# Moving the sample states' loads, copies and outer products inside the second feed-forward stage, and the normalisation's pinned steps at the end

## The chip, the cores and the metric

The kernel runs on one core of one Trainium2 chip. The time is device microseconds (us) of one execution of the whole program. TensorE (PE) multiplies matrices, with its weight loads shown as a row of their own (PEld); VectorE (DVE), ScalarE (ACT) and GpSimd (POOL) compute elementwise; SyncE (SP), ACT and POOL issue DMA transfers. Each engine works through its own instructions in order, and engines wait for each other by semaphores.

## The reference

One layer of a decoder for 512 new prompt tokens and 8 sample tokens (one new token for each of 8 sequences). With `h` the residual stream (1024 features):

```python
h = h + 0.5 * swiglu(rms_norm(h, ffn1_norm), w_gate, w_up, w_down)      # FFN 1, 2816 wide
h = h + hybrid_mixer(rms_norm(h, mix_norm), ...)                         # pooling and state-space mixer
h = h + 0.5 * swiglu(rms_norm(h, ffn2_norm), w_gate, w_up, w_down)      # FFN 2
y = rms_norm(h, final_norm)
```

The mixer keeps a state for each sample sequence b and each of 16 heads, of 64 x 128 numbers (1024 rows of 128 for each b). One step of it is

```python
new_state = exp(dt * A) * old_state + outer(dt * x, B)      # per sequence and head
```

The output `new_ssm_sample` is this new state, 4 MB of float32 for all 8 sequences; nothing later in the step reads it. All outputs are float32.

## The kernel before

**Layout.** Features lie on the 128 partitions and the 520 tokens (512 prompt, 8 sample) in the free dimension, cut in two halves of 260 (`HALVES`, `HB`). A float32 operand is split into a high part (fp32r) and a low rest, and one product is three matmuls (`mm3`, lines 122, 125 and 126). The two FFNs also save one of eight sub-products by a seven-product scheme (Strassen's).

**An FFN's steps.** The class `Ffn` works through 22 blocks of 128 hidden features in four chunks. For each chunk it takes the gate and up products of its blocks (tiles named `A_k` and `BE_k`, weights `raw`, `whi`, `wlo`, `shi`, `slo`), and then the down products of the chunk, two output blocks at a time (the same names with `1d` or `2d`: four down tiles for each of the first three chunks). Below, a "gate tile" is a step with 7 x 12 matmul groups and a "down tile" one with 7 x 9. The border of a chunk is where its last gate tile gives way to its first down tile.

`step(k)` (line 426 on) writes one tile: product 1, a call of `state()`, product 4 of the tile before, then products 5, 6, 3, 7 and 2, with another `state()` after product 3. Products 1, 6, 7 and 4 pile up in one PSUM bank (`A`), products 5 and 3 in another (`BE`); between them ACT copies the running sum out (`ac`, line 361), and the next product of that bank may not start before its copy. A product's weights come from SP's loads (`raw`), ACT's casts (`whi`, `shi`, line 106), DVE's differences (`wlo`, `slo`, line 113) and, for parts of `wlo`, an ACT write of the negative (line 109) to which a POOL DMA adds the weight itself from memory (line 110). The gates of a tile run on DVE (lines 373, 379, 382, 387) and ACT (the SiLU, line 380), and the hidden values are split for the down products by `g_split` (lines 257 to 266; the wide cast is L265 over 1040 columns, followed by DVE's L266).

**What sets the order.** The program is recorded in the order of the code, and a planner that runs a timeline model orders each engine's instructions when the program is built; instructions wrapped in `keep_in_program_order` (`pin`) stay in the code's order among themselves on their engine. So a moved call moves other instructions too.

**The sample states.** `new_states` (line 903 on) is a generator that `state()` advances by one piece at a time: two pieces for each of 32 halves, one half being two of the four 128-row blocks that share one row B (a sequence has two such groups of four). The first piece is POOL's: the accumulate of the previous half (`out_nss<-so`, line 920, a DMA that adds `so` to what lies in memory), every second half the row B spread over the partitions (`br`, line 923, from `scr_bc`), and the load of the next half's old state (`hs`, line 913). The second piece is ACT's: two scaled copies of the old state in place (line 931), a DMA of ACT's queue that writes them to the output (line 932, `out_nss<-hs`), and two outer products (`so`, line 935: `br` scaled per partition). `so` and `br` have one buffer each, `hs` two. The accumulate must wait until the copy of its half has landed in memory.

**The end.** The last chunk's down products run token half by token half (`down_by_half`). As each output block d is done, `after2` (line 611) takes its squares; `finish` sums them over the partitions by a matmul with ones (`psl`), takes the root on ACT, and queues in `todo` the pinned steps of DVE: two reciprocals (line 642) and four scalings `hg * r` of two blocks each (line 646), every scaling followed by a store of `y`. `after2` takes one of these from `todo` at every block of the second token half, and the rest at the end, after the second half's `finish`.

Of the kernel before, what the change touches and what calls it, by code (L numbers as in the profile page):

```python
# [9 lines left out]
F32 = mybir.dt.float32  # L10
F32R = mybir.dt.float32r
AF = mybir.ActivationFunctionType
# [4 lines left out]
P = 128  # L17
# [4 lines left out]
HB = NT // 2  # L22
# [39 lines left out]
def tile_trunk_step(ctx: ExitStack, tc: tile.TileContext, ins: dict, outs: dict):  # L62
    nc = tc.nc
# [7 lines left out]
    tmp = ctx.enter_context(tc.tile_pool(name="tmp", bufs=3, side="right"))  # L71
# [10 lines left out]
    def v(name, i, n=P):  # L82
        return vec[:n, VEC[name] + i : VEC[name] + i + 1]
# [64 lines left out]
    def sumsq(acc, d, hs, name):  # L148
        n = hs.stop - hs.start
        if d == 0:  # L150
            nc.scalar.activation(out=acc[:, hs], in_=h[:, d, hs], func=AF.Square)
        else:
            sq = tmp.tile([P, HB], F32, tag="ta", name=f"sq_{name}_{d}")
            nc.scalar.activation(out=sq[:, :n], in_=h[:, d, hs], func=AF.Square)
            nc.vector.tensor_tensor(out=acc[:, hs], in0=acc[:, hs], in1=sq[:, :n], op=ALU.add)
# [48 lines left out]
    class Ffn:  # L204
# [221 lines left out]
        def step(self, k):  # L426
            if k not in self.A:
                self.product(k, 1)
            self.state()
            self.flush()  # L430
            for p in (2, 5, 6, 3, 7) if k == KF - 1 else (5, 6, 3, 7, 2):
                self.product(k, p)
                if p == 3:
                    self.state()
            self.gates(k)
            self.pending = k

# [86 lines left out]
    for j in range(KD // 2):  # L524
        for d in (j, j + KD // 2):
            q = slice(NVEC + d * NT if d else 0, NVEC + (d + 1) * NT)
# [82 lines left out]
    todo, late = [], []  # L609

    def after2(d, b, hs):
        hg, _, last = res
        if (d, b) == (0, 1):
            finish(0, [last[:, HALVES[0]]])
        elif b and todo:
            todo.pop(0)()
        if b and d >= KD - 2:
            late.append(tmp.tile([P, HB], F32, tag="ta", name=f"sq_last{d}"))
            nc.scalar.activation(out=late[-1], in_=h[:, d, hs], func=AF.Square)
        else:  # L620
            sumsq(last, d, hs, f"l{d}{b}")
        if (d, b) == (KD - 1, 1):
            nc.vector.tensor_scalar(out=hg[:, d, hs], in0=h[:, d, hs], scalar1=v("final_norm", d), scalar2=None,
                                    op0=ALU.mult)
            finish(1, [last[:, hs], *late])
            while todo:
                todo.pop(0)()
            return
        nc.scalar.activation(out=hg[:, d, hs], in_=h[:, d, hs], func=AF.Copy, scale=v("final_norm", d))

    def finish(b, sqs):
        hs, hg, rl, _ = HALVES[b], *res
        ps = bank(f"psl{b}")
        for k, sq in enumerate(sqs):
            nc.tensor.matmul(ps[:, :HB], ones, sq, start=k == 0, stop=k == len(sqs) - 1)
        cuts = (0, HB // 2, HB)
        quarters = [slice(cuts[i], cuts[i + 1]) for i in range(2)]
        for q in quarters:
            nc.scalar.activation(out=rl[:, hs][:, q], in_=ps[:, q], func=AF.Sqrt, bias=eps, scale=1.0 / D)

        def inverse(q):
            tc.keep_in_program_order(nc.vector.reciprocal(out=rl[:, hs][:, q], in_=rl[:, hs][:, q]))

        def out(d):
            tc.keep_in_program_order(
                nc.vector.tensor_tensor(out=hg[:, d : d + 2, hs], in0=hg[:, d : d + 2, hs],
                                        in1=rl[:, hs].unsqueeze(1).to_broadcast([P, 2, HB]), op=ALU.mult))
            nc.sync.dma_start(out=outs["y"][:, d : d + 2, hs], in_=hg[:, d : d + 2, hs])

        todo.extend([lambda q=q: inverse(q) for q in quarters])  # L650
        todo.extend([lambda d=d: out(d) for d in range(0, KD, 2)])

    f2["ffn"].rest(before2, after2)
    for p in (ps[0], f2["st"], g2, f2["hg"], f2["wx"]):
        p.release()


def mixer(tc, ins, outs, e):
    nc = tc.nc
    cst, act, wp, tmp, dr, pool = (e[x] for x in ("cst", "act", "wp", "tmp", "dr", "pool"))  # L660
# [4 lines left out]
    xh, xl, _, r = nx2[0]  # L665
# [184 lines left out]
    sxdt = cst.tile([P, NX, NS], F32, tag="sxdt", name="sxdt")  # L850
# [5 lines left out]
    def rows_bc(b, a, g):  # L856
        return scr_bc.rearrange("b (a g n) -> b a g n", a=2, g=2)[b, a, g].unsqueeze(0).to_broadcast([P, P])
# [45 lines left out]
    def new_states(sp):  # L903
        todo = [(b, g, q) for g in range(2) for b in range(NS) for q in (0, 2)]
        pin = tc.keep_in_program_order

        def js(t, i):
            b, g, q = todo[i]
            return t[:, b, 4 * g + q : 4 * g + q + 2]

        def load(i):
            t = sp.tile([P, 2, P], F32, tag="sh", bufs=2, name=f"hs{i}")
            pin(nc.gpsimd.dma_start(out=t, in_=js(ins["state_ssm"], i)))  # L913
            return t

        ahead, last, br = load(0), None, None
        for i, (b, g, q) in enumerate(todo):
            yield
            if last is not None:
                pin(nc.gpsimd.dma_start(out=js(outs["nss"], i - 1), in_=last, accum_op=ALU.add))  # L920
            if q == 0:
                br = sp.tile([P, P], F32, tag="sb", name=f"br{i}")
                pin(nc.gpsimd.dma_start(out=br, in_=rows_bc(b, 0, g)))
            hs = ahead
            if i + 1 < len(todo):
                ahead = load(i + 1)
            yield
            last = sp.tile([P, 2, P], F32, tag="so", name=f"so{i}")
            for u in range(2):
                j = 4 * g + q + u  # L930
                pin(nc.scalar.activation(out=hs[:, u], in_=hs[:, u], func=AF.Copy, scale=sdec[:, j, b : b + 1]))
            pin(nc.scalar.dma_start(out=js(outs["nss"], i), in_=hs))
            for u in range(2):
                j = 4 * g + q + u
                pin(nc.scalar.activation(out=last[:, u], in_=br, func=AF.Copy, scale=sxdt[:, j, b : b + 1]))  # L935
        yield
        pin(nc.gpsimd.dma_start(out=js(outs["nss"], len(todo) - 1), in_=last, accum_op=ALU.add))

# [268 lines left out]
```

## Time and profile before

| what | before |
|---|---|
| median of 3 runs | 999.99 us (999.51 to 1001.24) |
| profiled execution | 999.96 us, span 997.9 us |
| PE / PEld busy | 956.7 us (96%) / 929.4 us (93%) |
| DVE / ACT / POOL busy | 866.5 / 676.2 / 230.8 us |
| outer products `so` (L935) | 64, 22.2 us busy, 25.1 us idle before them |
| accumulates `out_nss<-so` | 32, landing after 6.2 us (median) |
| PE busy from 40 to 335 us (FFN 1) | 291.66 of 295 us |
| PE busy from 640 to 965 us (FFN 2) | 312.73 of 325 us |

Reading it: the first FFN runs to about 340 us, the mixer to about 640 us, the second FFN from there to the end. A row of the timeline gives start, duration, engine, line, operation, tiles and, in brackets, the idle time of the engine just before and what ended it. A row of the waits gives who waited for whom: total us, times, longest. PEld's idle time is the better measure of a stop of TensorE, since weights are loaded one ahead of the matmul.

### The profile page before, as it was taken

The page shows a single profiled execution, that of the slowest core. Times are in us where ns is not written, and L with a number is a line of the kernel's source. Part 1 is how long each engine was busy: PE and PEld are TensorE (multiplying, and loading weights), DVE is VectorE, ACT ScalarE, POOL GpSimd, SP SyncE. Part 2 cuts the span into 40 slices and gives each one's busy share as a digit, 9 for nine tenths or more (in the row PEclk, how much of TensorE's full clock was granted, in tenths as well). Part 3 has the DMA queues.
Part 4 walks back from the last instruction along what each step waited for, and adds up shares of the span by engine and source line. Part 5 has one row for each costly group of instructions (what it writes and reads, how often), then busy time and mean ns, then how long its engine had stood idle before and what let it go on. Part 6 is the DMA issues. An engine that isn't in the chain of part 4 may idle for free.

```text
span 997.9 us, 20209 instructions
## 1 busy us (share of the span) xinstructions
PE 956.7 (96%) x7636; PEld 929.4 (93%) x7636; DVE 866.5 (87%) x1580; ACT 676.2 (68%) x1251; POOL 230.8 (23%) x319
## 2 busy tenths in 40 slices
PE   7999999999999999999999999999999999999995
PEld 6899999999999999999899989899899998999994
DVE  7998999989988688698989987999879987998875
ACT  7676777777767565675844235778768877887753
POOL 0111211221121000158212000133433333343300
PEclk9999999999999999999999999999999999999998
DMA  5565766576566242453244321478788787887832
GB/s 186 153 167 113 204 150 153 127 183 163 128 157 150 75 156 86 125 184 118 92 146 136 134 85 54 124 184 191 172 196 216 165 204 201 199 185 184 187 79 86
DMA packets 71249, 149.65 MB, mean 150 GB/s; under 512 B 9768, under 2 KB 31208, under 8 KB 71152
## 3 DMA queue, kind: packets, MB, share of 16 engines
q1 hardware_dynamic: 41168, 103.78, 33.2%
q0 software_dynamic: 25376, 40.38, 23.0%
q10 hardware_dynamic: 4608, 4.20, 1.3%
q8 instruction: 60, 0.98, 0.4%
q14 instruction: 37, 0.30, 0.1%
HBM read 136.80 MB, written 11.53 MB: 149 GB/s over the span
## 4 chain that ended last, share of the span: by engine, by line
PE 71%; DVE 9%; DMA 7%; ACT 6%; issue 4%; POOL 1%; SPq 0%; ACTq 0%; DVEq 0%; POOLq 0%
PE A L122 7%; PE A L126 6%; PE A L125 6%; PE BE L122 5%; PE BE L125 5%; PE BE L126 5%; PE P L292 3%; DMA br<-scr_bc 3%; DMA out_nss<-so 2%; PE wo L122 2%; PE wo L126 2%; PE wo L125 2%; PE inz L122 2%; PE A1d L126 2%; PE A1d L122 2%
## 5 line engine op out<-in xcount | busy, mean ns | idle before, releaser
L361 ACT COPY ac<-A 128x260 f32<-128x260 f32 x123 | 44.5, 371 | 16.2 <-PE A L126 16.0
L292 PE MATMUL P<-xg_f,raw 128*128 128x260 f32 x192 | 45.6, 395 | 5.7 <-DMA raw<-in_w1gu 5.2
L327 DVE TENSOR_TENSOR s<-raw 128x1024 f32<-128x1024 f32 x41 | 49.9, 1218 | 0.0
L292 PEld LDWEIGHTS P<-xg_f,raw 128*128 128x128 f32 x192 | 37.3, 197 | 11.7 <-ACT xg_f L188 5.2
L935 ACT ACTIVATE so<-br,sxdt 128x128 f32<-128x128 f32 x64 | 22.2, 394 | 25.1 <-DMA br<-scr_bc 16.6
L125 PE MATMUL wo<-catg,whi_wo 128*128 128x260 f32 x128 | 36.4, 285 | 1.3 <-DVE catg L1064 1.3
L122 PE MATMUL wo<-catg,whi_wo 128*128 128x260 f32 x128 | 37.3, 293 | 0.3 <-DVE h L1033 0.3
L106 ACT CAST whi_wo<-raw_wo 128x1024 fp32r<-128x1024 f32 x12 | 12.5, 1046 | 36.5 <-issue 9.2
L122 PE MATMUL inz<-xh_mx,whi_inz 128*128 128x260 f32 x128 | 36.8, 288 | 0.1
L122 PE MATMUL inx<-xh_mx,whi_inx 128*128 128x260 f32 x128 | 36.5, 285 | 0.0
L126 PE MATMUL wo<-catg,wlo_wo 128*128 128x260 f32 x128 | 36.4, 285 | 0.0
L126 PE MATMUL inx<-xh_mx,wlo_inx 128*128 128x260 f32 x128 | 36.2, 283 | 0.0
L126 PE MATMUL inz<-xh_mx,wlo_inz 128*128 128x260 f32 x128 | 36.2, 283 | 0.0
L125 PE MATMUL inz<-xl_mx,whi_inz 128*128 128x260 f32 x128 | 36.2, 283 | 0.0
L125 PE MATMUL inx<-xl_mx,whi_inx 128*128 128x260 f32 x128 | 36.2, 283 | 0.0
L920 POOL DMA_DIRECT2D out_nss<-so x31 | 34.1, 1102 | 6.0 <-DMA out_nss<-hs 4.8
L913 POOL DMA_DIRECT2D hs<-in_state_ssm x32 | 34.5, 1079 | 3.4 <-DVE xtl_f L202 2.6
L373 DVE TENSOR_TENSOR tg<-BE,ac 128x520 f32<-128x520 f32 x41 | 28.5, 694 | 4.5 <-PE BE L126 3.8
L787 DVE SCALAR_TENSOR_TENSOR A<-U,h,A 128x544 f32<-128x544 f32 x36 | 28.1, 781 | 4.2 <-ACT A L785 3.9
L382 DVE TENSOR_TENSOR tg<-tg,r_f 128x520 f32<-128x520 f32 x41 | 28.6, 697 | 1.5 <-ACT tg L380 1.3
L379 DVE TENSOR_TENSOR tg<-tg,r_f 128x520 f32<-128x520 f32 x41 | 28.5, 696 | 0.1
L361 ACT COPY ac<-BE 128x260 f32<-128x260 f32 x41 | 15.3, 373 | 19.3 <-PE BE L126 14.1
(1787 smaller groups left out, 4764.3 us busy)
## 6 DMA issues: line engine op xcount, KB each, us to landing
raw<-in_w2gu SPq DMA_DIRECT2D x44, 512.0 KB, 4.4
raw<-in_w1gu SPq DMA_DIRECT2D x42, 512.0 KB, 4.6
raw_1d<-in_w1d SPq DMA_DIRECT2D x24, 384.0 KB, 3.9
raw_2d<-in_w2d SPq DMA_DIRECT2D x24, 384.0 KB, 3.7
raw_wo<-in_w_out SPq DMA_DIRECT2D x12, 512.0 KB, 4.6
ab<-scr_acs SPq DMA_DIRECT2D x8, 512.0 KB, 4.5
h<-in_state_ssm SPq DMA_DIRECT2D x16, 256.0 KB, 4.1
raw_inz<-in_w_in SPq DMA_DIRECT2D x8, 512.0 KB, 3.9
```

Source lines behind the costliest of these rows:

```text
L122: first = nc.tensor.matmul(ps, whi, xhi, start=start, stop=False, **kw)
L125: nc.tensor.matmul(ps, whi, xlo, start=False, stop=False, **kw)
L126: nc.tensor.matmul(ps, wlo, xhi, start=False, stop=stop, **kw)
L292: nc.tensor.matmul(self.banks[f, u][b][:, :HB], ws(self.raw[f][:, u], j + 4 * q), xg[:, slot[q]], start=j == q == 0, stop=j == 3 and q == ...
L327: nc.vector.tensor_tensor(out=s1, in0=diag, in1=up0, op=ALU.add)
L361: nc.scalar.copy(keep, out[:, :HB])
L373: nc.vector.tensor_tensor(out=tg, in0=self.BE[k][:, :, :HB], in1=a, op=ALU.add)
L379: nc.vector.tensor_tensor(out=tg, in0=tg, in1=r, op=ALU.mult)
L382: nc.vector.tensor_tensor(out=tg, in0=tg, in1=r, op=ALU.mult)
L787: nc.vector.scalar_tensor_tensor(out=A[:, :n], in0=U[:, j : j + n], scalar=w(j), in1=A[:, :n], op0=ALU.mult, op1=ALU.add)
L913: pin(nc.gpsimd.dma_start(out=t, in_=js(ins["state_ssm"], i)))
L920: pin(nc.gpsimd.dma_start(out=js(outs["nss"], i - 1), in_=last, accum_op=ALU.add))
```

## The change

It has three parts.

1. In `step`, the second `state()` is called after all of the tile's products, not after product 3. So ACT's piece of a half is recorded behind the tile's product 2, and its POOL piece stays where it was.
2. In `new_states`, the row `br` is loaded by `row(i)`, into one of two buffers and two halves before its first use, and it is issued behind the load of `hs`, not ahead of it. The outer products `so` are written into the tiles with the tag `ta` (three buffers, which also hold squares at other times), no longer into one buffer of their own.
3. In `after2`, the pinned steps of the end are taken from `todo` only from block d = 3 of the second token half on, not from d = 1.

```diff
@@ -430,8 +430,7 @@ step
             self.flush()
             for p in (2, 5, 6, 3, 7) if k == KF - 1 else (5, 6, 3, 7, 2):
                 self.product(k, p)
-                if p == 3:
-                    self.state()
+            self.state()
             self.gates(k)
             self.pending = k
 
@@ -612,7 +611,7 @@ after2
         hg, _, last = res
         if (d, b) == (0, 1):
             finish(0, [last[:, HALVES[0]]])
-        elif b and todo:
+        elif b and todo and d > 2:
             todo.pop(0)()
         if b and d >= KD - 2:
             late.append(tmp.tile([P, HB], F32, tag="ta", name=f"sq_last{d}"))
@@ -913,26 +912,33 @@ new_states
             pin(nc.gpsimd.dma_start(out=t, in_=js(ins["state_ssm"], i)))
             return t
 
-        ahead, last, br = load(0), None, None
+        def row(i):
+            b, g, _ = todo[i]
+            t = sp.tile([P, P], F32, tag="sb", bufs=2, name=f"br{i}")
+            pin(nc.gpsimd.dma_start(out=t, in_=rows_bc(b, 0, g)))
+            return t
+
+        rows, ahead, last = [row(0)], load(0), None
         for i, (b, g, q) in enumerate(todo):
             yield
             if last is not None:
                 pin(nc.gpsimd.dma_start(out=js(outs["nss"], i - 1), in_=last, accum_op=ALU.add))
-            if q == 0:
-                br = sp.tile([P, P], F32, tag="sb", name=f"br{i}")
-                pin(nc.gpsimd.dma_start(out=br, in_=rows_bc(b, 0, g)))
             hs = ahead
             if i + 1 < len(todo):
                 ahead = load(i + 1)
+            if q == 0 and i + 2 < len(todo):
+                rows.append(row(i + 2))
             yield
-            last = sp.tile([P, 2, P], F32, tag="so", name=f"so{i}")
+            last = tmp.tile([P, HB], F32, tag="ta", name=f"so{i}")[:, : 2 * P].rearrange("p (u n) -> p u n", u=2)
             for u in range(2):
                 j = 4 * g + q + u
                 pin(nc.scalar.activation(out=hs[:, u], in_=hs[:, u], func=AF.Copy, scale=sdec[:, j, b : b + 1]))
             pin(nc.scalar.dma_start(out=js(outs["nss"], i), in_=hs))
             for u in range(2):
                 j = 4 * g + q + u
-                pin(nc.scalar.activation(out=last[:, u], in_=br, func=AF.Copy, scale=sxdt[:, j, b : b + 1]))
+                pin(nc.scalar.activation(out=last[:, u], in_=rows[0], func=AF.Copy, scale=sxdt[:, j, b : b + 1]))
+            if q:
+                rows.pop(0)
         yield
         pin(nc.gpsimd.dma_start(out=js(outs["nss"], len(todo) - 1), in_=last, accum_op=ALU.add))
```

## The prediction

> **What bounds the kernel.** I read the page first (busy shares, then the chain that ended last), then who TensorE waits for, and then the timeline of ACT, POOL and DVE around those waits.
>
> ```profile
> PE 71%; DVE 9%; DMA 7%; ACT 6%; issue 4%; POOL 1%; SPq 0%; ACTq 0%; DVEq 0%; POOLq 0%
> ```
>
> TensorE (96% busy) carries 71% of the chain, and 7% hang on DMAs. The two FFNs do the same work on the same tiles, but only the second carries the sample states. So the same matmul at each of the three chunk borders, in FFN 1 and in FFN 2, gives the states' price (timeline of PE, start first):
>
> ```profile
> 91.92 0.39 PE L122 MATMUL BE1d<-gt,shi_1d_0c 128*128 128x260 f32 x1 [1.03 <-ACT gt L265]
> ...
> 185.11 0.39 PE L125 MATMUL BE1d<-gt,shi_1d_1c 128*128 128x260 f32 x1 [0.47 <-DVE gt L266]
> ...
> 277.16 0.39 PE L125 MATMUL BE1d<-gt,shi_1d_2c 128*128 128x260 f32 x1 [0.47 <-DVE gt L266]
> ...
> 704.50 0.39 PE L122 MATMUL BE2d<-gt,shi_2d_0c 128*128 128x260 f32 x1 [1.04 <-ACT gt L265]
> ...
> 801.84 0.39 PE L125 MATMUL BE2d<-gt,shi_2d_1c 128*128 128x260 f32 x1 [0.43 <-DVE gt L266]
> ...
> 897.28 0.39 PE L125 MATMUL BE2d<-gt,shi_2d_2c 128*128 128x260 f32 x1 [0.43 <-DVE gt L266]
> ```
>
> The first chunk takes 93.19 us in FFN 1 and 97.34 in FFN 2, the second 92.05 and 95.44: 4.15 and 3.39 us more. The waits of the weight loads name the cause. Behind the first border, from 705.5 to 966 us:
>
> ```profile
> PEld A2d L122 <- ACT ac2d L361: 7.1, 6, 1.9
> PEld A L122 <- ACT ac L361: 1.9, 3, 0.7
> ...
> PEld A2d L122 <- ACT shi_2d_0d L106: 1.1, 1, 1.1
> ```
>
> That is 10.1 us: nine stops, three behind each of the three borders, and one cast. The two chunks between borders give 7.5 of it by the clock on the wall, which leaves about 3 for the third. One of these stops in the timelines of ACT, PE and POOL, with ACT's two largest waits on DMAs between 640 and 965 us:
>
> ```profile
> 727.24 0.69 ACT L935 ACTIVATE so<-br,sxdt 128x128 f32<-128x128 f32 x2 [2.41 <-DMA br<-scr_bc]
> ...
> 729.39 0.64 ACT L361 COPY ac2d<-A2d 128x260 f32<-128x260 f32 x2
> ```
> ```profile
> 729.80 0.39 PE L122 MATMUL A2d<-gt,whi_2d_0b 128*128 128x260 f32 x1 [1.52 <-ACT ac2d L361]
> ...
> 738.82 0.39 PE L122 MATMUL A2d<-gt,whi_2d_0b 128*128 128x260 f32 x1 [0.46 <-ACT ac2d L361]
> ```
> ```profile
> 729.06 0.88 POOL L110 DMA_DIRECT2D wlo_2d_0b<-in_w2d  x1 [4.90 <-ACT wlo_2d_0b L109]
> ```
> ```profile
> ACT so L935 <- DMA br<-scr_bc: 16.6, 9, 2.5
> ...
> ACT so L935 <- DMA out_nss<-so: 6.9, 8, 1.4
> ```
>
> ACT stands in order behind an outer product that waits for its row B. The copy of product 7 comes late, and product 4, which may not enter the bank before it, stops TensorE. From 729.80 to 738.82 TensorE runs 69 matmuls beside the 0.46 of the next stop: 0.12 us each, so a down tile (63) takes 7.5 us without a stop.
>
> **The change part by part.**
>
> *Rows early, and outer products in the three buffers `ta`.* Both waits of `so` lose their cause. The landing times between 640 and 965 us:
>
> ```profile
> out_nss<-hs ACTq DMA_DIRECT2D x32, 128.0 KB, 3.9
> out_nss<-so POOLq DMA_DIRECT2D x32, 128.0 KB, 6.2
> hs<-in_state_ssm POOLq DMA_DIRECT2D x30, 128.0 KB, 5.8
> br<-scr_bc POOLq DMA_DIRECT2D x15, 64.0 KB, 5.9
> ...
> wlo_2d_1b<-in_w2d POOLq DMA_DIRECT2D x4, 192.0 KB, 5.6
> ```
>
> A row issued two halves ahead has two tiles, at least 15 us, for its 5.9, and a buffer used again after three halves has been read out long since (6.2). The load of `hs`, now ahead of the row, is if anything earlier. No instruction or byte is added, and SP's queue issues the same transfers in the same order.
>
> *ACT's piece behind the tile's last product.* Per half, the two scaled copies, the DMA they issue on ACT's queue and the two outer products leave the place between product 6's copy and the weight casts. In the changed program the copies stand right behind product 7's copy, the outer products behind the next tile's product 1 copy. What is late next is that tile's product 5 copy: two pairs like the 0.69 above and three copies of 0.32 make 2.3 us behind product 7, and product 3 needs it only four products later (1, 5, 4, 6), at 36 x 0.12 = 4.3 us in a down tile. So it is hidden. I take all 10.1 us; the bounds are 0 and 10.1. The 1.1 on `shi_2d_0d` goes as well, since this cast no longer has the state's pieces ahead of it.
>
> *POOL.* The copy to memory is issued about two products later, and the accumulate waits for its landing. Behind the accumulate in POOL's queue stand the next `hs`, a row, and the DMA into the next tile's last `wlo`. That one is issued now 9.8 us ahead of its use (729.06 for 738.82) and lands after 5.6, so it can be some 4 us later. The load of `hs` has two tiles. I take 0; the bounds are 0 and 6 (the first rival).
>
> *The chunk borders.* The changed order of ACT puts the last gate tile's SiLU and a weight cast ahead of the wide cast `gt` (L265) at all three borders of FFN 2; before, it stood so only at the first. The weight loads' waits at the first border (700 to 709 us) and the second (799 to 804), and two ACT rows of the first:
>
> ```profile
> PEld BE2d L122 <- ACT gt L265: 1.3, 1, 1.3
> PEld A2d L122 <- DVE gx L387: 0.5, 1, 0.5
> PEld BE2d L122 <- ACT ac2d L361: 0.4, 1, 0.4
> ...
> PEld BE2d L125 <- DVE gt L266: 0.6, 1, 0.6
> PEld BE2d L122 <- ACT ac2d L361: 0.4, 1, 0.4
> ```
> ```profile
> 701.48 0.64 ACT L380 ACTIVATE tg<-tg 128x520 f32<-128x520 f32 x1 [0.24 <-DVE tg L379]
> 702.65 0.84 ACT L106 CAST whi_2d_0a<-raw_2d 128x768 fp32r<-128x768 f32 x1 [0.54 <-PE A L125]
> ```
>
> 2.2 us against 1.0: two borders get 1.2 dearer, **+2.4**. The outer products (0.69) now stand ahead of the SiLU too, but ACT idles 0.24 + 0.54 there. The bounds are 0 and 2.4 + 3 x 1.4 = 6.6, if both pairs fell on the path.
>
> *The start of FFN 2.* Waits of weight loads from 643 to 662 us, and ACT:
>
> ```profile
> PEld A L122 <- ACT ac L361: 0.5, 1, 0.5
> PEld A L126 <- DVE slo_1d L113: 0.4, 1, 0.4
> ```
> ```profile
> 644.83 1.05 ACT L106 CAST shi_1c<-s 128x1024 fp32r<-128x1024 f32 x1
> ```
>
> These 0.9 us go, as nothing of a state then stands ahead of that work. But `shi_1c` moves behind the outer products (0.69) and two casts of half its own length, and two of its matmuls move ahead of product 3: an estimate of 1.0 us, between 0 and 0.69 + 1.05 = 1.7. **+0.1** net.
>
> *The end.* DVE, PE, and the granted clock in windows of 982.7 to 985.5 and 985.5 to 988.6 us (the number behind the busy times):
>
> ```profile
> 982.29 1.92 DVE L646 TENSOR_TENSOR hg<-hg,r_last 128x520 f32<-128x520 f32 x3
> 984.12 0.42 DVE L504 TENSOR_TENSOR h<-dh,h 128x260 f32<-128x260 f32 x1
> ...
> 985.06 0.42 DVE L155 TENSOR_TENSOR acc_last<-acc_last,sq_l 128x260 f32<-128x260 f32 x1
> ```
> ```profile
> 985.54 1.23 PE L635 MATMUL psl<-acc_last,ones 128*128 128x260 f32 x2 [2.84 <-DVE acc_last L155]
> 986.57 1.94 PE L635 MATMUL psl<-sq_last,ones 128*128 128x260 f32 x4
> ```
> ```profile
> 982.70:985.50 2.80, 0.01 (x1) 0.00 (x0) 2.80 (x7) 1.07 (x3) 0.00 (x0) 0.95 0.55 184
> 985.50:988.60 3.10, 2.97 (x6) 1.84 (x6) 0.68 (x2) 0.47 (x2) 0.00 (x0) 0.50 0.53 178
> ```
> ```profile
> L292 PE MATMUL P<-xg_f,raw 128*128 128x260 f32 x192 | 45.6, 395 | 5.7 <-DMA raw<-in_w1gu 5.2
> ```
>
> Before, three scalings of 0.61 stand ahead of block 6's sum `h`; in the changed order there is one, and the others stand behind blocks 6 and 7. The squares are ready 1.2 us sooner, and TensorE's gap shrinks from 2.84 to 1.6 us. After the long gap its clock was 0.50, and six matmuls took 2.97 us; at full clock the same shape takes 45.6 / 192 = 0.24. The 1.52 us gap at 729.80 was followed by matmuls at full speed. So I expect the full clock: `psl` from 984.3, its last pair (after block 7's square, near 985.2) done by 985.9, not 988.5. **-2.6**; the bounds are -1.2 (clock still half) and -2.6. The two postponed scalings end near 986.0, before the root is back.
>
> [...]
>
> *Sum:* -10.1 + 2.4 + 0.1 - 2.6 = -10.2 us. The profiled execution took 999.96 us (span 997.9, 2.1 around it), the median 999.99: no correction. **989.8 us.**
>
> **The rivals.**
>
> *POOL takes over the wait.* The copy leaves two products later (18 x 0.12: 2.2 us), and should it land like an accumulate (6.2, not 3.9), POOL is held 2.3 us more. Together 4.5, against the 4 us that the last `wlo` can take: product 4 would wait about 0.5 us in each of 12 down tiles, 6 us in all, 995.8. For it: POOL's queue is one line, and every accumulate in it waits for a copy. Against: the casts ahead of that DMA come earlier by 1.4 us, and gate tiles have a third more time. [...] 16%.
>
> *Late `hs` stops ACT (slower).* The scaled copies now stand ahead of the next tile's `ac` copies. If an old state lands late, ACT stands, and products 6 and 3 with it. Copy landing plus load take 3.9 + 5.8 + about 1.7 for issues = 11.4 us, against two down tiles of some 7.5 = 15; with the 1.5 us or more that product 5's copy has to spare, it decides from 16.5 us on. At 1 us beyond in 12 tiles the gain of 10.2 is gone and 2 more: 1001.8. 7%.
>
> *The change moves no wait.* If the 1.4 us of state work, and not the row's wait, makes the `ac` copies late, they are late again at the next product: the 10.1 stay, and 999.96 + 2.4 + 0.1 - 2.6 = 999.9. Against: stops come where `so` waited and nowhere else. 7%.
>
> **How the numbers follow.** Forecast 70%, its own range 987 to 992 (from no loss at the borders, 987.4, to half a clock at the end, 991.2, and a dearer start). With the first rival it reaches to 996.5; outside stay the other two. A measurement of this kernel can tell about 0.2% (2 us) from no change. Faster by over 0.2%: 70 + 16 = 86%; within: 7%; slower: 7%.
>
> **What would show it.** Right: no wait of `so` on `br` or on its own accumulate; no weight load waiting for `ac2d` or `ac` inside a chunk; about 93 us between the borders of FFN 2; three waits for `gt` L265 there; `psl` with the clock at 1.00. Wrong: TensorE waiting for `wlo` or a DMA, ACT waiting for `hs`, or the SiLU on the path at the borders.

## The result

The changed kernel is slower: 1015.79 us in the median (1011.58 to 1017.79) against 999.95 before, a ratio of 1.0151 with a 95% interval of 1.0117 to 1.0184. The forecast was 989.8. The profiled execution took 1016.24 us (span 1014.1), 16.2 us of span more than before. In its chain of work the DMAs have grown from 7 to 12%:

```profile
PE 71%; DMA 12%; DVE 8%; issue 3%; ACT 3%; POOL 2%; SPq 0%; DVEq 0%; POOLq 0%; ACTq 0%
```

The same matmuls at the three borders of FFN 2 as before (timeline of PE, changed kernel):

```profile
708.04 0.39 PE L122 MATMUL BE2d<-gt,shi_2d_0c 128*128 128x260 f32 x1 [1.05 <-ACT gt L265]
...
816.63 0.34 PE L125 MATMUL BE2d<-gt,shi_2d_1c 128*128 128x260 f32 x1
...
918.47 0.35 PE L125 MATMUL BE2d<-gt,shi_2d_2c 128*128 128x260 f32 x1
```

The chunks take 108.59 and 101.84 us, where 93 was expected and 97.34 and 95.44 had been measured. The way to the first border has grown by 3.5 us, and behind the last the changed kernel is 5.0 us faster (1014.1 - 918.47 = 95.6 against 997.9 - 897.28 = 100.6). The waits of the weight loads from 640 us to the end tell what replaced what:

```profile
PEld BE2d L126 <- DMA wlo_2d_0a<-in_w2d: 4.6, 1, 4.6
PEld BE2d L122 <- ACT gt L265: 3.8, 3, 1.3
PEld BE L126 <- DMA wlo_15a<-in_w2gu: 2.4, 1, 2.4
PEld BE L126 <- DMA wlo_8a<-in_w2gu: 2.4, 1, 2.4
...
PEld BE L122 <- ACT shi_1c L106: 2.0, 1, 2.0
```

The 7.1 us of `A2d` waiting for `ac2d` are gone. In their place stand twelve waits for a `wlo` (the three rows shown and nine smaller ones from 2.2 to 0.3, 19.2 us in all), eleven of them in gate tiles, one in a down tile. Not one of them is for the `wlo` of product 4 that the prediction looked at. POOL's accumulates, from the groups of the page, before and after:

```profile
L920 POOL DMA_DIRECT2D out_nss<-so x31 | 34.1, 1102 | 6.0 <-DMA out_nss<-hs 4.8
```
```profile
L925 POOL DMA_DIRECT2D out_nss<-so x31 | 27.4, 883 | 166.9 <-DMA out_nss<-hs 92.2
```

POOL's idle time ahead of them, waiting for the copy to land, went from 4.8 to 92.2 us. One half shows the whole way. Its copy belongs to the step of tile 7, and the accumulate that waits for it stands in POOL's queue ahead of the first `wlo` of tile 8 (the tiles run 7, 10, 8). Before (timelines of ACT, POOL and PE):

```profile
750.88 1.05 ACT L106 CAST whi_10a<-raw 128x1024 fp32r<-128x1024 f32 x1 [0.60 <-PE A L125]
...
753.98 0.34 ACTq L932 DMA_DIRECT2D out_nss<-hs  x1
...
758.85 0.87 POOL L920 DMA_DIRECT2D out_nss<-so  x1 [0.55 <-DMA out_nss<-hs]
...
763.65 0.90 POOL L110 DMA_DIRECT2D wlo_8a<-in_w2gu  x1 [2.81 <-ACT ac L361]
...
774.16 0.29 PE L126 MATMUL BE<-xth_f,wlo_8a 128*128 128x260 f32 x1
```

And after:

```profile
758.53 1.05 ACT L106 CAST whi_10a<-raw 128x1024 fp32r<-128x1024 f32 x1 [0.51 <-PE A L125]
...
767.41 0.34 ACTq L936 DMA_DIRECT2D out_nss<-hs  x1
...
775.30 0.87 POOL L925 DMA_DIRECT2D out_nss<-so  x1 [9.68 <-ACT gt L265]
...
777.52 0.94 POOL L110 DMA_DIRECT2D wlo_8a<-in_w2gu  x1
...
784.45 0.39 PE L126 MATMUL BE<-xth_f,wlo_8a 128*128 128x260 f32 x1 [2.15 <-DMA wlo_8a<-in_w2gu]
```

Measured from the same weight cast, the copy leaves after 3.10 us before and after 8.88 now: 5.8 us later, not 2.2. It also lands later (landing times of these two copies, first before, then after):

```profile
out_nss<-hs ACTq DMA_DIRECT2D x1, 128.0 KB, 4.3
```
```profile
out_nss<-hs ACTq DMA_DIRECT2D x1, 128.0 KB, 7.3
```

The accumulate in POOL's queue cannot pass before the copy has landed, and POOL now idles 9.68 us ahead of it. The profile puts this wait down to a cast of ACT that the accumulate does not read; the copy lands at 767.41 + 7.3 = 774.7, as the cast ends, and 18 other accumulates name the copy. Behind it stand `hs`, a row and `wlo_8a`. Before, this `wlo` was issued 10.5 us ahead of its use in the bank `BE`; now 4.8 us ahead of the moment at which TensorE wants it (784.45 - 2.15 = 782.30). Its landing time, too, grew:

```profile
wlo_8a<-in_w2gu POOLq DMA_DIRECT2D x1, 256.0 KB, 3.7
```
```profile
out_nss<-hs ACTq DMA_DIRECT2D x31, 128.0 KB, 6.2
...
wlo_8a<-in_w2gu POOLq DMA_DIRECT2D x1, 256.0 KB, 6.9
```

(landing times from 640 to 965 us; first before, then after). 6.9 against 4.8 us gives the 2.1 us stop. In gate tiles POOL now releases, after most of these waits, four or five transfers within 3 us, so that they are under way side by side (the five around tile 8 were issued from 775.30 to 778.09 us; `wlo_8a` landed after 6.9 us, `wlo_8b` after 7.7).

The stops cost more than their length. Windows of 5 us after six of them in the changed kernel (the number behind the busy times is the granted clock):

```profile
648.00:653.00 5.00, 4.76 (x27) 4.76 (x28) 4.16 (x7) 2.09 (x5) 1.94 (x3) 0.66 0.71 182
723.50:728.50 5.00, 5.00 (x29) 5.00 (x30) 2.45 (x4) 2.08 (x5) 2.29 (x3) 0.66 0.60 90
784.40:789.40 5.00, 4.95 (x28) 4.95 (x29) 2.96 (x6) 1.75 (x3) 2.53 (x4) 0.66 0.87 132
852.20:857.20 5.00, 4.99 (x29) 4.99 (x30) 2.44 (x3) 1.56 (x3) 2.88 (x4) 0.66 0.78 104
886.90:891.90 5.00, 4.95 (x28) 4.95 (x29) 3.27 (x6) 1.75 (x3) 3.17 (x4) 0.66 0.65 108
751.40:756.40 5.00, 5.00 (x41) 5.00 (x42) 3.30 (x4) 3.10 (x7) 2.00 (x4) 1.00 0.56 128
```

Five of the six run at a clock of 0.66 in the mean, so 5 x (1 - 0.66) x 2 = 3.4 us at half speed (a clock of 0.50, as in the stretch from 784.93 us in the last section); they hold 27 to 29 matmuls where a full-speed window holds 41. That is an estimate of 13 x 0.12 = 1.6 us each, 8 us in all. The ledger by the waits of weight loads: 30.8 us after against 20.4 before from 640 us on, +10.4; half clock +8 here and, with no half clock at the end any more, -1.4: +17.0, against 16.2 of span.

### The profile page after: what moved, and what is told of

Its sections match the earlier page's. It is cut to its first block, busy times and chain, and to the rows that moved or that the text cites. A ratio compares the mean times of both kernels' runs of the same rounds, so it can differ in the third digit from the quotient of the medians.

```text
span 1014.1 us, 20189 instructions
## 1 busy us (share of the span) xinstructions
PE 963.5 (95%) x7636; PEld 936.4 (92%) x7636; DVE 869.7 (86%) x1580; ACT 678.5 (67%) x1251; POOL 228.7 (23%) x319
## 4 chain that ended last, share of the span: by engine, by line
PE 71%; DMA 12%; DVE 8%; issue 3%; ACT 3%; POOL 2%; SPq 0%; DVEq 0%; POOLq 0%; ACTq 0%
PE A L125 5%; PE A L122 5%; PE A L126 5%; PE BE L126 5%; PE BE L122 4%; PE BE L125 4%; PE P L292 3%; DMA out_nss<-hs 2%; PE wo L122 2%; PE wo L126 2%; PE wo L125 2%; PE inz L122 2%; PE A1d L126 2%; PE A1d L122 2%; PE A1d L125 2%
## 5 line engine op out<-in xcount | busy, mean ns | idle before, releaser
L925 POOL DMA_DIRECT2D out_nss<-so x31 | 27.4, 883 | 166.9 <-DMA out_nss<-hs 92.2
L912 POOL DMA_DIRECT2D hs<-in_state_ssm x32 | 28.3, 885 | 0.0
L328 DVE TENSOR_TENSOR s<-s,raw 128x512 f32<-128x512 f32 x41 | 28.0, 683 | 0.0
L329 DVE TENSOR_TENSOR s<-s,raw 128x512 f32<-128x512 f32 x41 | 27.9, 682 | 0.0
```

The source lines that it names most:

```text
L328: nc.vector.tensor_tensor(out=s2[:, 0], in0=s1[:, 1], in1=raw[:, 0, :nb], op=ALU.add)
```

## The experiments

**The three parts one by one.** Part 1 alone (`e1_late_call`), part 2 alone (`e2_rows`), part 3 alone (`e3_end`), and parts 2 and 3 (`e4_rows_end`). Edits against the kernel before, the first three in one diff:

```diff
@@ e1 step
-                if p == 3:
-                    self.state()
+            self.state()
@@ e2 new_states
 (the changed kernel's new_states, whole)
@@ e3 after2
-        elif b and todo:
+        elif b and todo and d > 2:
```

> Part 1 alone: the second state() behind all products, rows and outer products as before. Theory A (the copy leaves ACT some 5 us later in the tile, the accumulate holds POOL's queue until it has landed, and the first wlo of the next tile comes late): the whole loss is here and the gain of the end is missing, so 1018 us (1015.8 + 2.6), with over 80 us of POOL waiting for out_nss<-hs. The row br, still in that queue behind the accumulate, may add to it. Theory B (the loss comes from the rows and outer products, by other DMA traffic or the shared buffers ta): no loss here, 990 to 1000 us.

> Part 2 alone: rows two halves ahead, outer products in ta, state() behind product 3 as before. Theory A: both waits of so go, POOL's queue keeps its small wait (4.8 us in all), and most of the 10.1 us of late copies go: 991 to 995 us. Theory B: the loss of the changed kernel is here: 1010 us or more.

> Part 3 alone: the pinned steps from block 3 on. By the prediction's step for the end: 997.4 us (-2.6), the last psl at full clock. If the end in the changed kernel was short only because something before it was late: 1000 us.

> Parts 2 and 3 without part 1. Theory A: the gains of the two add, 988 to 992.5 us, faster than both kernels, with no weight load of TensorE waiting for a wlo. Theory B: slower than before, 1008 us or more.

| kernel | median, us | ratio to before, 95% interval |
|---|---|---|
| part 1 | 1047.96 | 1.046 (1.0408 to 1.0512) |
| part 2 | 989.82 | 0.99 (0.9877 to 0.9922) |
| part 3 | 998.71 | 0.9987 (0.9977 to 0.9997) |
| parts 2 and 3 | 987.69 | 0.9877 (0.9851 to 0.9902) |

Part 3 alone lies between the two times that were expected for it, and parts 2 and 3 just below their range. The whole loss lies in part 1. Alone it costs 48 us, far more than the 18 expected (1018 us). The rows, and the one buffer of `so`, then stand behind the held accumulate (ACT's largest waits from 640 us on, and the largest of the weight loads):

```profile
ACT so L934 <- DMA br<-scr_bc: 28.3, 8, 5.2
ACT so L934 <- DMA out_nss<-so: 22.9, 5, 5.9
```
```profile
PEld BE L122 <- ACT ac L361: 22.6, 7, 4.5
```

The waits of the weight loads add up to 52.6 us there against 20.4 before, and between 640 us and the gap at the end TensorE runs 37.5 us at half clock, against 17 in the changed kernel and none in the kernel before.

Beside parts 2 and 3 the late call costs 28.1 us (1015.79 - 987.69), so part 2 shelters it from some 20. Part 2 alone gains 10.1 us, more than the 5 to 9 expected, and part 3 on top of it 2.1. With parts 2 and 3 the largest waits of weight loads in FFN 2 are these, and no `wlo` and no `A2d` waiting for `ac2d` is among them:

```profile
PEld psl L635 <- DVE acc_last L155: 1.8, 1, 1.8
PEld A L126 <- DVE slo_1d L113: 1.5, 1, 1.5
PEld BE2d L122 <- ACT ac2d L361: 1.3, 3, 0.4
...
PEld BE2d L122 <- ACT gt L265: 1.2, 1, 1.2
```

Theory B falls: rows and buffers cost nothing.

**The accumulate one half later, then a third home for `hs`.** Both keep the late call of part 1 and take away what POOL waits for. First only the accumulate (`e5_acc_later`), then also the load of `hs` (`e10_third_home`), against the changed kernel (shortened: the empty list `outer` at the start and the last two accumulates at the end are not shown):

```diff
@@ e5 new_states
-            if last is not None:
-                pin(nc.gpsimd.dma_start(out=js(outs["nss"], i - 1), in_=last, accum_op=ALU.add))
+            if len(outer) == 2:
+                pin(nc.gpsimd.dma_start(out=js(outs["nss"], i - 2), in_=outer.pop(0), accum_op=ALU.add))
...
+            outer.append(last)
@@ e10, on top of e5
-            t = sp.tile([P, 2, P], F32, tag="sh", bufs=2, name=f"hs{i}")
+            t = sp.tile([P, 2, P], F32, tag="sh", bufs=3, name=f"hs{i}")
...
-            t = sp.tile([P, P], F32, tag="sb", bufs=2, name=f"br{i}")
+            home = (cst, "ident") if i % 4 else (sp, "sb")
+            t = home[0].tile([P, P], F32, tag=home[1], name=f"br{i}")
```

> The changed kernel, with each accumulate issued one half later, so that its copy has a whole tile more to land before POOL's queue reaches the accumulate. Theory A (POOL stands for the copy's landing): the 92.2 us of POOL's wait for out_nss<-hs go, with them the 19.2 us of weight loads waiting for a wlo and the spells of half clock behind them (some 6 us): 987 to 993 us, and what is then left above the kernel with parts 2 and 3 alone (987.7) is the price of part 1 at the borders (2.4) and at the start. Theory C (the copies in their new place collide with the weight loads, whose landing rose from 3.7 to 6.5 us for raw_2d): the accumulate's place changes little, 1005 us or more.

> The changed kernel with each accumulate one half later and a third buffer for hs (the second row's buffer is the mixer's idle identity tile), so that nothing in POOL's queue waits any more for the copy just issued. Theory A: POOL's 64.1 us of waiting for out_nss<-hs, now ahead of the load of hs, go, and the last 4.1 us of weight loads waiting for a wlo and the one spell of half clock with them: 989 to 991 us, and what stays above 986.6 to 987.7 is part 1 at the borders and at the start. Theory C (late copies collide with the weight loads): wlo waits stay, 994 us or more.

With the accumulate later, 995.25 us (ratio 0.9941, 0.9919 to 0.9962): most of the loss is gone, though less than expected. The wait had only moved one place on in POOL's queue (waits of POOL; then of weight loads):

```profile
POOL hs L912 <- DMA out_nss<-hs: 64.1, 18, 6.9
```
```profile
PEld BE L126 <- DMA wlo_8a<-in_w2gu: 2.3, 1, 2.3
...
PEld BE L126 <- DMA wlo_14a<-in_w2gu: 1.0, 1, 1.0
PEld BE L126 <- DMA wlo_12a<-in_w2gu: 0.8, 1, 0.8
```

The load of the next `hs` goes into the buffer from which the copy is still being written out, so it stood for the same copy. The third buffer takes that away too: 992.41 us (0.9924, 0.9896 to 0.9952), still a little above the 989 to 991 expected, but POOL waits only 5.1 us for a copy, and no `wlo` is waited for:

```profile
POOL out_nss L926 <- DMA out_nss<-hs: 5.1, 3, 2.1
```
```profile
PEld BE2d L122 <- ACT gt L265: 3.7, 3, 1.2
PEld BE L122 <- ACT shi_1c L106: 2.0, 1, 2.0
PEld psl L634 <- DVE acc_last L155: 1.8, 1, 1.8
PEld A2d L126 <- DVE slo_2d_2d L113: 1.7, 1, 1.7
PEld A2d L126 <- DVE slo_2d_1d L113: 1.4, 1, 1.4
```

Theory A is shown: some 23 us of the changed kernel (1015.79 - 992.41) hang on POOL's wait for the copy. Theory C falls. The copies still land after 6.0 us here (median from 640 to 960 us), but nothing waits for them, and the weight loads `raw_2d`, whose landing had risen from 3.7 to 6.5 us, are back at 3.7, so that rise did not come from the copies' new place either. What remains is the price of part 1 with hardly a wait of POOL: 4.6 us of span over parts 2 and 3 (990.6 against 986.0), on the borders (`gt`), the start (`shi_1c`) and differences of DVE that wait for casts of ACT (`slo_2d`). The late call gives nothing back for it.

**Rows or buffers.** Both have parts 2 and 3 without part 1, but one half of part 2 undone: all outer products in one tile (`e7_rows_only`), or the row loaded as before (`e8_buffers_only`). The lines of e7 are against parts 2 and 3, those of e8 against part 3 alone.

```diff
@@ e7 new_states
-            last = tmp.tile([P, HB], F32, tag="ta", name=f"so{i}")[:, : 2 * P].rearrange("p (u n) -> p u n", u=2)
+            if last is None:
+                last = tmp.tile([P, HB], F32, tag="ta", name="so")[:, : 2 * P].rearrange("p (u n) -> p u n", u=2)
@@ e8 new_states
-            last = sp.tile([P, 2, P], F32, tag="so", name=f"so{i}")
+            last = tmp.tile([P, HB], F32, tag="ta", name=f"so{i}")[:, : 2 * P].rearrange("p (u n) -> p u n", u=2)
```

> Parts 2 and 3 without part 1, but all outer products in one tile, as in the kernel before: only the rows are loaded ahead. If the late rows (16.6 us of ACT's wait) make the stops of TensorE, nearly the whole gain stays: 987.5 to 989.5 us. If the wait for the buffer (6.9 us) does, most of it is lost: 994 to 998 us.

> Parts 2 and 3 without part 1, but the row loaded as in the kernel before (one buffer, behind the accumulate): only the outer products have three buffers. If the late rows make the stops, they stay: 995 to 998.5 us. If the buffer's wait makes them, 988 to 991 us.

The rows alone gain nothing: 998.64 us (0.9982, 0.9973 to 0.9992), the time of part 3 alone. The buffers alone gain about half: 993.80 (0.9931, 0.9916 to 0.9945). Together they reach 987.69. ACT's largest wait in the one and in the other:

```profile
ACT so L941 <- DMA out_nss<-so: 22.5, 16, 2.4
```
```profile
ACT so L935 <- DMA br<-scr_bc: 15.5, 9, 3.0
```

In the kernel before, ACT waited 16.6 us for rows and 6.9 for the buffer. With the row early, the buffer's wait does not stay at 6.9 but takes the whole place, 22.5. The buffer is free only when the accumulate has landed, after 6.2 us in the kernel before, and the row, issued some 0.5 us behind it, lands after 5.9. My expectation, which read the two sums as separable, was wrong on both runs.

**A better version.** The first row stood ahead of the first old state in POOL's queue, and ACT waited 3.2 us for `hs` at the start of FFN 2 with parts 2 and 3. `e9_state_first` swaps them; `e11_end_later` also moves the pinned steps one block further.

```diff
@@ e9 new_states, on parts 2 and 3
-        rows, ahead, last = [row(0)], load(0), None
+        ahead, rows, last = load(0), [row(0)], None
@@ e11 after2, on top of e9
-        elif b and todo and d > 2:
+        elif b and todo and d > 3:
```

> Parts 2 and 3 without part 1, and the first old state loaded ahead of the first row: ACT's 3.2 us of waiting for hs at the start of the second FFN go, and with them the 1.25 us that TensorE waits for slo_1d there: 986.5 us. If that wait has another cause: 987.7 us, no change.

> Parts 2 and 3 without part 1, first old state ahead of first row, and the pinned steps of the end only from block 4 on. TensorE's gap ahead of the last psl shrinks from 1.6 to about 1.0 us, but the scaling that moves back stands ahead of the reciprocals, where DVE has only some 0.25 us to spare: 986.3 us. If the postponed scalings fall on the path: 986.9 us.

986.56 us (0.9856, 0.9840 to 0.9873), with ACT's wait for `hs` gone and TensorE's for `slo_1d` down from 1.5 to 0.5: faster than both kernels, 14.2 us below the runs of the kernel before that stood beside it (1000.76) and 29 below the changed one. The further step is 986.93 (0.9867, 0.9852 to 0.9881), no difference that can be told.

## Why the prediction was wrong

- **The step that failed is *POOL*: "I take 0".** It priced the later copy at nothing by three statements, each too small. "About two products later" (2.2 us) is three products in the order of ACT, from product 6's copy to the tile's last, and a gate product has 12 matmul groups, not 9: 5.8 us measured for the copy above, which also landed 3.0 us later. "Gate tiles have a third more time" looked at product 4's `wlo` only; the accumulate stands ahead of both `wlo` DMAs of a gate tile, and the first of them is needed 10.5 us after its issue and lands after 3.7, so 6.8 us to spare; it came later by 5.7 (4.8 instead of 10.5) and landed 3.2 later. And the landing times were taken as fixed, where `wlo_8a`, released with four others within 2.8 us, landed after 6.9 us instead of 3.7.
- **The first rival was the right mechanism with the wrong place and size.** It had POOL taking over the wait, at 16% and +6 us, in 12 down tiles. Measured: 19.2 us of stops, eleven of twelve in gate tiles, and, by the estimate above, over 6 us for the half clock behind four of them, which the rival did not count at all. With the pieces above it would have come out beyond the time before; so a forecast of "faster" with 86% stood on a price for one queue that had been worked out at one tile only.
- **The gain of 10.1 us was credited to the wrong part, and its size is in part luck.** Part 2 alone measures -10.1. The prediction put it to rows, buffers and the moved call together; the moved call adds nothing to it, since the stops of `A2d` and `A` on ACT's copies (7.1 + 1.9) go without it. The 1.1 on `shi_2d_0d` stays with part 2 alone; in its place the profile of that run has its last matmuls clear of the half clock that cost 1.4 us before (below).
- **The borders (+2.4) and `gt`:** three waits as forecast, 3.8 us against 1.3 before, less the two of `gt` L266 (1.3) that went, and 0.7 more for `gx`: +1.9.
- **The start (+0.1):** `shi_1c` cost 2.0 us, above the upper bound of 1.7, and a spell of half clock behind it in the profiled execution.
- **The end (-2.6):** the gap shrank to 1.6 us and `psl` ran at full clock as said, in the changed kernel's profile. As a difference of medians, part 3 alone is worth 1.3 us (0.3 to 2.3) and 2.1 on top of part 2. The profile of part 2 alone shows one reason why it is less than 2.6: there the long gap stands, and the matmuls behind it run almost at full clock (PE, then the window with the clock 0.95).

```profile
976.66 0.71 PE L635 MATMUL psl<-acc_last,ones 128*128 128x260 f32 x2 [2.83 <-DVE acc_last L155]
```
```profile
976.60:978.20 1.60, 1.54 (x6) 1.00 (x6) 0.70 (x3) 0.42 (x1) 0.00 (x0) 0.95 1.00 343
```

With part 1 alone, which keeps the old end too, the clock behind the same gap is 0.62 (1032.60 to 1035.70 us). So the half clock on `psl` was no fixed cost: two of three profiles with the old end have it, and its 1.4 us should have been counted as a chance. What the runs show of it stands in the last section.
- **The other rivals:** ACT waited for `hs` once, 0.9 us, so late `hs` was not the loss. "The change moves no wait" falls with part 2 alone.

## What to carry to other kernels

Before a transfer is moved to a later place, list what stands behind its waiter in that engine's queue, in every kind of tile, with issue, landing and use; take the smallest margin, and expect longer landings of what is then released together (here 6.9 instead of 3.7 us for `wlo_8a`). Where two waits follow each other on one engine, removing one may give nothing until the other goes too (here the rows alone: 998.64 us, against 998.71 with part 3 alone). Try the part that removes a wait's cause without the part that moves work around it.

## What the runs showed of the hardware

Half-speed spells of TensorE (a granted clock of 0.50) set in after stops of 1.75, 1.75, 2.15, 2.19 and 4.38 us in the changed kernel, but not after one of 1.98 in the same execution, nor after a stop at `shi_1c` of 1.77 us with the third home for `hs`:

```profile
647.90:652.90 5.00, 5.00 (x41) 5.00 (x42) 5.00 (x8) 3.40 (x6) 0.73 (x2) 1.00 0.84 215
```

In the changed kernel the clock drops at 648.39, 723.48, 784.92, 853.19 and 887.32 us. Each of these five spells lasts 3.413 us (the third from 784.922 to 788.335), and the distances between the drops, 75.09, 61.44, 68.27 and 34.13 us, are 22, 18, 20 and 10 times that. In the stretch of 3.41 us that ends at each drop, TensorE stood still for 1.75, 3.41, 2.15, 2.19 and 1.75 us. Such stretches, laid end to end through the drops, divide the stop of 1.98 us into 1.38 and 0.60. The one of 1.77 they divide into 0.72 and 1.05; this is an estimate, counted back in steps of 3.413 us from the drop of its own run at 984.73 us. Here are the two stretches of the 1.98, then the one with the stop of 2.15 and the one behind it (changed kernel; length, PE's busy time, and the clock as above):

```profile
747.37:750.78 3.41, 2.05 (x18) 1.84 (x16) 2.48 (x5) 1.83 (x3) 0.86 (x1) 1.00 1.06 244
750.79:754.20 3.41, 2.81 (x23) 2.81 (x24) 1.90 (x3) 1.16 (x2) 0.00 (x0) 1.00 0.59 107
781.51:784.92 3.41, 1.26 (x11) 1.05 (x9) 2.54 (x5) 1.57 (x2) 1.18 (x3) 1.00 0.80 145
784.93:788.33 3.40, 3.40 (x18) 3.40 (x17) 1.67 (x3) 1.15 (x2) 1.58 (x3) 0.50 0.90 137
```

Laid over the changed kernel from 15 us on, all other stretches have up to 1.62 us of standstill and a clock of 1.00 behind them, up to the end of the work; there one goes the other way, the stretch from 1003.38 to 1006.79 us, with 1.94 us of standstill behind the last matmul and a clock of 1.00 after it. In the kernel before, the stretch ahead of the drop at 985.23 us has 2.52 us, all earlier ones from 15 us on at most 1.35. With part 1 alone, the 37.5 us at half clock are 11.0 times 3.413. So whether a spell follows a stop went, in these runs, with where the stop lay among the stretches; what sets them, and from what standstill on a spell follows, no run shows. They do not lie at the same place against the work in each execution: with the old gap at the end, the drop comes at 985.23 us in the kernel before, ahead of all six matmuls of `psl` (985.54 on), and at 978.06 with part 2 alone, behind nearly all of them (976.66 on).

From 640 us on, five of the six stops of 1.75 us or more in the changed kernel have a spell behind them; in the kernel before, those of 1.47, 1.52 and 1.64 us in FFN 2 have none. In this kernel a stop as long as these five must therefore be counted with the risk of some 1.6 us more, by the estimate above.
